# Experts of a mixture in unsplit fp32 on groups of the array's width, with the schedule in two pieces

## The chip, the cores and the metric

The kernel runs on one core of one Trainium2 chip. The time is that of one launch in device microseconds. Before the change it is 1426.45 us, the median of three runs (1423.62 to 1427.33).

## The reference

A transformer step in fp32 for 512 tokens of width 1024, in two blocks. The first is an RWKV-7 mixer beside chunked band attention, with an adaptive norm ahead and an output product behind. The second has a hybrid mixer (state space, forgetting attention, convolution), then a mixture of 32 experts, and a last RMS norm. Only the mixture is changed:

```
p_g = softmax(h @ w_rg + b_rg);  g = argmax(p_g)            # one of 4 groups
top_p, top_i = top_k(softmax(logits of the 8 experts of g), 2)
weights = top_p / sum(top_p) * p_g[g]
for each expert e, on the rows of h that chose it:
    y = (silu(h @ w_gate[e]) * (h @ w_up[e])) @ w_down[e]   # 1024 -> 512 -> 1024
x = x + g_f * sum over a token's two experts of weight * y
out = rms_norm(x) * final_norm_g
```

Each expert has two matrices of 1024 x 512 and one of 512 x 1024 in fp32: 6.29 MB, and 201 MB for all 32. The 512 tokens with two experts each make 1024 rows, which the kernel keeps sorted by expert.

## The kernel before, in words

The kernel is not issued as it is written. A recorder (class `Recorder`, line 209) takes down every instruction with what it reads and writes. A planner (`schedule`, line 613) then simulates the engines with a price for each instruction (`cost`, line 425; 360 GB/s for a transfer) and fixes the order of each engine's queue. `arrange` (line 341) gives every tile a place in one of three areas of the on-chip memory: "f" of 34816 columns in fp32, "r" of 18176 in fp32r, "i" for integers. `build` runs this for the whole kernel as a single piece (line 2611 and following), then emits the instructions. On the chip each engine works through its own queue in that order. Behind it stands a loop for experts with more rows than a window holds; in the profiled execution it has no pass.

**Matmuls in split fp32r.** A factor in fp32 is cut into a high part, rounded to fp32r, and a low part, the difference. A product is then three fp32r matmuls: high by high, low by high, high by low. Each is one instruction on PE.

**Experts.** `expert_code` (line 2397) works on a window of 80 rows of the sorted table `hs`, which holds the 1024 rows transposed, as eight blocks of 128 of the width. It copies the window (ACT, high part; DVE, low part). Then come eight pieces of weights of 128 x 1024 elements (0.5 MB each), gate and up in turn. For each, the high part is copied by ACT or DVE and the low part subtracted by DVE, and PE runs six matmuls with the 80 rows as the stationary operand. After the gate (Tanh on ACT, two fused operations on DVE) the 80 x 512 hidden values are transposed on PE in four parts and split again. Four more pieces hold the down matrix, for another 24 matmuls. The two halves of the result are multiplied by the channel gate `gfb` on DVE, and POOL scatters the rows to the table `Yd` in HBM by row numbers from `sli`; rows past an expert's count have a number out of bounds and are skipped.

```
RAW, HIS, LOS = 14, 6, 6        # line 979
PRE = 14
R.copy(hi, raw)                 # in Rings.split, line 2390
R.tt(lo, raw, hi.bitcast(F32), ALU.subtract)
```

**Weights held.** `Rings` holds 14 pieces in area "f" and 6 high and 6 low parts in area "r". SP loads a piece as soon as the plan has it and the buffer is free, which it is once the two instructions of the split have read it. The first 14 pieces (`PRE`) are loaded ahead of the second mixer's output product.

**Routing.** After the output product the router's logits are transposed (`lg`), and DVE works out group, experts, weights and each row's place in a chain of small instructions. One-hot matrices (`SS`, compared with the row `iota`) and PE give the token numbers in sorted order. POOL gathers eight blocks of 128 rows of the normalized x from HBM (`Xd`), and PE transposes them into `hs`. Expert 0 needs the first block only, expert 1 rows up to 592, the others possibly all.

**The end.** The last two experts are staggered (`AHEAD`, line 981). The result of expert 31 doesn't go through HBM: selection matrices (`selt`, split) times its rows are added to x in PSUM by 24 matmuls. The rows of the others are gathered from `Yd` by POOL, two gathers for each block of 128 tokens. Then come the last norm and the writes of the output.

## Time and profile before

| | us |
|---|---|
| median of 3 runs | 1426.45 |
| lowest, highest | 1423.62, 1427.33 |
| the profiled execution, its own time | 1425.2 |
| its span in the trace | 1423.4 |
| PE busy, PEld busy | 1323.5, 921.0 |
| DVE busy, ACT busy, POOL busy | 1195.8, 834.7, 191.1 |
| weight pieces loaded by SP | 384 of 512 KB |

PE is TensorE's matmuls, PEld its weight loads (they may overlap), DVE VectorE, ACT ScalarE, POOL GpSimd and SP SyncE, which only issues transfers here. The profile is one execution. The span runs from its first to its last instruction, and times in it count from its start. Experts fill the span from about 790 to 1395 us. An fp32 matmul shows as two instructions, an fp32r matmul as one, and both show as "f32" in the shapes; the areas tell them apart ("areaf" is area "f", "arear" area "r"). Nearly all instructions have line 965, where the planned instructions are emitted.

### The profile page before, as it was taken

Reading aid. Unit: us, or ns where it says so; the run is one execution under the profiler, and the core shown is the slowest. Engines: PE = TensorE matmul, PEld = TensorE weight load, DVE = VectorE, ACT = ScalarE, POOL = GpSimd, SP = SyncE. Lnnn points to the kernel's source line nnn. Section 1 sums busy time; section 2 is a strip of 40 time slices with the busy share of each in tenths; the row PEclk is TensorE's granted clock in tenths of the full one; section 3 lists DMA queues with packets and bytes.
Section 4 is the critical chain, followed back from the end, with each engine's and each line's share of the span. In section 5 each row is a group of like instructions: output and inputs, shape, how many; then the busy total and the mean of one; then the engine's idle time right before and its main releaser. Section 6 shows DMA issues by size and latency. Waiting matters only on the chain. (4 is left out here: it accounts for less than half of the span.)

```text
span 1423.4 us, 21185 instructions
## 1 busy us (share of the span) xinstructions
PE 1323.5 (93%) x7400; PEld 921.0 (65%) x7400; DVE 1195.8 (84%) x2183; ACT 834.7 (59%) x1327; POOL 191.1 (13%) x126
## 2 busy tenths in 40 slices
PE   5999999999989989999998899999999999999993
PEld 2766566676757888878886556666556565555552
DVE  5496966679789474999947889999999999999995
ACT  5454634456484254366723578876766677667662
POOL 0000000000001000000101201221523710001123
PEclk8999999999999999999998799999999999999997
DMA  9734766400205511000534689999999999999955
GB/s 334 283 99 147 248 249 222 141 16 17 74 17 164 190 54 55 26 15 2 196 131 148 210 292 364 371 354 364 345 354 357 345 356 359 345 344 339 354 189 182
DMA packets 90739, 307.74 MB, mean 216 GB/s; under 512 B 12034, under 2 KB 15490, under 8 KB 89604
## 3 DMA queue, kind: packets, MB, share of 16 engines
q1 hardware_dynamic: 85252, 293.75, 56.8%
q0 software_dynamic: 5376, 12.59, 2.5%
q8 instruction: 59, 0.97, 0.3%
q14 instruction: 52, 0.43, 0.1%
HBM read 293.72 MB, written 18.87 MB: 220 GB/s over the span
## 5 line engine op out<-in xcount | busy, mean ns | idle before, releaser
L965 PE MATMUL ps<-arear 128*80 128x512 f32 (+3 forms) x4435 | 1063.1, 391 | 44.3 <-DVE areaf L965 17.5
L965 PEld LDWEIGHTS ps<-arear 128*80 128x80 f32 (+1 forms) x4435 | 701.7, 171 | 334.3 <-issue 32.0
L965 ACT ACTIVATE arear<-areaf 128x1024 fp32r<-128x1024 f32 (+7 forms) x542 | 496.8, 944 | 275.2 <-PE ps L965 203.1
L965 DVE TENSOR_TENSOR arear<-areaf,arear 128x1024 fp32r<-128x1024 f32 (+5 forms) x560 | 598.3, 1105 | 50.5 <-PE ps L965 21.5
L965 PE MATMUL ps<-areaf 128*32 128x128 f32 (+18 forms) x2965 | 340.5, 315 | 34.8 <-DVE areaf L965 23.3
L965 PEld LDWEIGHTS ps<-areaf 128*128 128x128 f32 (+7 forms) x2965 | 233.0, 144 | 146.9 <-issue 49.9
L957 POOL DMA_INDIRECT yscr<-areaf,areai x32 | 134.2, 4194 | 434.6 <-DVE areaf L965 404.8
L965 ACT ACTIVATE areaf<-ps 128x512 f32<-128x512 f32 (+7 forms) x294 | 118.6, 421 | 121.1 <-PE ps L965 108.7
L965 ACT ACTIVATE areaf<-areaf 128x512 f32<-128x512 f32 (+9 forms) x246 | 121.4, 512 | 105.9 <-DVE areaf L965 96.2
L965 DVE TENSOR_TENSOR areaf<-ps,areaf 128x512 f32<-128x512 f32 (+6 forms) x245 | 123.4, 513 | 13.4 <-PE ps L965 9.9
L965 DVE SCALAR_TENSOR_TENSOR areaf<-areaf 128x512 f32<-128x512 f32 (+6 forms) x190 | 108.2, 598 | 20.5 <-ACT areaf L965 18.0
L965 DVE TENSOR_TENSOR areaf<-areaf 128x512 f32<-128x512 f32 (+12 forms) x235 | 102.4, 450 | 9.9 <-ACT areaf L965 6.2
L965 DVE SCALAR_TENSOR_TENSOR areaf<-ps,areaf 128x511 f32<-128x511 f32 (+8 forms) x116 | 56.7, 502 | 44.7 <-PE ps L965 39.1
L965 ACT ACTIVATE areaf<-ps,areaf 128x128 f32<-128x128 f32 (+3 forms) x109 | 53.6, 517 | 42.2 <-PE ps L965 24.5
L965 POOL MEMSET areaf<- 128x512 f32 (+10 forms) x53 | 17.2, 331 | 427.8 <-DVE areaf L965 201.4
L965 POOL TENSOR_TENSOR areaf<-areaf 128x4 f32<-128x4 f32 (+2 forms) x21 | 19.9, 971 | 317.4 <-DVE areaf L965 301.7
L965 DVE TENSOR_SCALAR areaf<-areaf 128x256 f32<-128x256 f32 (+12 forms) x192 | 48.1, 280 | 9.8 <-ACT areaf L965 4.3
L965 DVE CAST arear<-areaf 128x1024 fp32r<-128x1024 f32 (+3 forms) x69 | 39.0, 568 | 13.4 <-PE ps L965 12.3
L965 DVE SCALAR_TENSOR_TENSOR areaf<-areaf,ps 80x512 f32<-80x512 f32 (+1 forms) x72 | 48.7, 677 | 0.1
L965 ACT ACT_TABLE_LOAD x35 | 44.9, 1283 | 1.3 <-PEq L2570 0.7
L965 DVE COPY areaf<-ps 32x128 f32<-32x128 f32 (+10 forms) x51 | 19.0, 375 | 23.4 <-ACT areaf L965 12.2
L965 ACT ACTIVATE arear<-ps 128x320 fp32r<-128x320 f32 (+1 forms) x36 | 14.8, 417 | 30.2 <-PE ps L965 30.1
(30 smaller groups left out, 182.1 us busy)
## 6 DMA issues: line engine op xcount, KB each, us to landing
areaf<-in_wx_dram SPq DMA_DIRECT2D x384, 512.0 KB, 5.6
areaf<-in_wada_dram SPq DMA_DIRECT2D x56, 512.0 KB, 4.6
areaf<-in_win_c_dram SPq DMA_DIRECT2D x43, 512.0 KB, 4.5
areaf<-in_wada_dram SPq DMA_DIRECT2D x8, 1024.0 KB, 8.2
areaf<-in_wout_dram SPq DMA_DIRECT2D x16, 512.0 KB, 4.1
areaf<-in_xt_dram SPq DMA_DIRECT2D x16, 256.0 KB, 3.5
yscr<-areaf SPq DMA_DIRECT2D x8, 512.0 KB, 8.2
areaf<-in_win_c_dram SPq DMA_DIRECT2D x24, 128.0 KB, 7.1
```

The lines of the kernel that those rows point to most:

```text
L957: self.emitted[i] = self.nc.gpsimd.indirect_dma_start(un(a[0]), bass.IndirectOffsetOnAxis(ap=un(k["idx"]), axis=0), un(k["in_"]), None, bo ...
L965: self.emitted[i] = getattr(getattr(self.nc, eng), op)(*[un(v) for v in a], **{n: un(v) for n, v in k.items()})
```

## The change

- Experts run in unsplit fp32: no copies, no subtractions, no high and low rings. Each window grows from 80 to 96 rows and is treated as a group of 64 and a group of 32.
- The group of 64 rows is the stationary operand of two matmuls that stand side by side in PE's columns: up in columns 0 to 63 and gate in 64 to 127, each over 512 columns of weights. The down product puts its two halves of 512 side by side likewise.
- The group of 32 rows stands four times side by side, each over 256 columns: both halves of up and of gate, then the four quarters of the down product.
- Results lie on 128 partitions as half and quarter rows. They are scattered by two scatters with their own tables `sl2` and `sl4`, in rows of 512 and 256 elements. The channel gate is spread accordingly (`g2`, `g4`).
- The last expert (31) keeps whole rows for its down product: a 64- and a 32-column matmul into the same bank, and one table `sl1`.
- The router's counting and the one-hot products, and the final selection, are in fp32 instead of fp32r.
- The schedule is cut: `trace` ends once `lg`, the transposed x and the writes to `Xd` are recorded, and `moe` is recorded, planned and emitted as a second piece. For it the columns of area "r" become an fp32 area "g", which holds `hs`, pieces and the last rows.
- The ring of weights is 30 pieces: the 14 loaded in the first piece, 8 in "g", 8 in "f". A piece's buffer is free once PE has read it.
- The planner's rate of transfers becomes 395 GB/s, and its price of a scatter smaller.

```diff
-RAW, HIS, LOS = 14, 6, 6
-PRE = 14
+PRE, MOREW = 14, "g" * 8 + "f" * 8
+RATE = 395.0
-WIN = 80
+WIN = 96
-R_WIDTH = 52992 - F_WIDTH
+R_WIDTH = 52928 - F_WIDTH
...
-    loaded = [rings.load(T["wx"][p]) for p in pieces[:PRE]]
+    loaded = []
+    for p in expert_pieces()[1][:PRE]:
+        loaded.append(R.tile([128, 1024], F32, "xraw"))
+        R.sync.dma_start(loaded[-1], T["wx"][p])
...
+    return dict(C={k: C[k] for k in keep}, loaded=loaded, lg=lg, xs=xs_, Xd=Xd, G3=G3, SH3=SH3, gf=A["gf"][0:64], nhalf=nhalf)
+def moe(R, T, S):
...
-    tid = R.tile([128, NT, 2], F32R, "tid")
+    tid = R.tile([128, NT, 2], F32, "tid")
...
-        gh, gl = R.tile([WIN, 1024], F32R, "ygh"), R.tile([WIN, 1024], F32R, "ygl")
...
-                R.tensor.matmul(p, lhsT=hi, rhs=gh[:, c], start=False, stop=False)
-                R.tensor.matmul(p, lhsT=hi, rhs=gl[:, c], start=False, stop=False)
-                R.tensor.matmul(p, lhsT=lo, rhs=gh[:, c], start=False, stop=(e == NEXP - 1))
+                R.tensor.matmul(p, lhsT=places[e, t], rhs=ys[:, c], start=False, stop=(e == NEXP - 1))
...
-def expert_code(R, C, hs, Yd, rings, gfb):
+def expert_code(R, C, hs, Yd, rings, g2, g4):
+    up, gate = slice(0, 64), slice(64, 128)
+    quarters = [slice(32 * g, 32 * g + 32) for g in range(4)]
...
-        R.scalar.activation(whi, a, AF.Copy)
-        R.vector.tensor_tensor(wlo, b, whi.bitcast(F32), ALU.subtract)
-        p = [bank("pg")[0:WIN], bank("pu")[0:WIN]]
-        for q in range(8):
-            hi, lo = rings.split(piece(q))
...
-                R.tensor.matmul(p[u], lhsT=whi[:, k], rhs=a, start=(k == 0), stop=False)
-                R.tensor.matmul(p[u], lhsT=wlo[:, k], rhs=a, start=False, stop=False)
-                R.tensor.matmul(p[u], lhsT=whi[:, k], rhs=b, start=False, stop=(k == KD - 1))
+        p, p4 = bank("pg"), bank("pg4")[:, 0:256]
+        for q in range(0, 8, 2):
+            g, u = piece(q), piece(q + 1)
             for kk in range(2):
+                k, c = q + kk, 512 * kk
+                with R.together():
+                    for o, w in ((up, u), (gate, g)):
+                        mm(p[o], lhsT=hw[:, k, 0:64], rhs=w[:, c:c + 512], start=(k == 0), stop=(k == KD - 1), tile_position=(0, o.start))
+            for kk in range(2):
+                k = q + kk
+                with R.together():
+                    for n, o in enumerate(quarters):
+                        c = 512 * kk + 256 * (n % 2)
+                        mm(p4[o], lhsT=hw[:, k, 64:96], rhs=(u, g)[n // 2][:, c:c + 256], start=(k == 0), stop=(k == KD - 1), tile_position=(0, o.start))
...
+        if whole:
+            py = [bank("py")[0:WIN], bank("py")[0:WIN]]
+            for k in range(4):
+                w = piece(8 + k)
+                for n in range(2):
+                    with R.together():
+                        for o, l in zip((slice(0, 64), slice(64, WIN)), part(k)):
+                            mm(py[n][o], lhsT=l, rhs=w[:, 512 * n:512 * n + 512], start=(k == 0), stop=(k == 3), tile_position=(0, o.start))
...
+        R.tt(ys, py, g2, ALU.mult)
+        R.tt(ys4, py4, g4, ALU.mult)
+        R.scatter(Yd.rearrange("r (h c) -> (r h) c", h=2), idx[0], ys, 2047)
+        R.scatter(Yd.rearrange("r (h c) -> (r h) c", h=4), idx[1], ys4, 4095)
...
+        areas = {"f": areas["f"], "g": pool.tile([128, R_WIDTH], F32, name="areag", tag="arear"), "i": areas["i"]}
+        R1, S = phase(lambda R, S: moe(R, T, S), S)
```

## Rows read from the trace of the kernel before

**Rows 1.** The page's first part: busy us (share of the span) and count by engine

```profile
PE 1323.5 (93%) x7400; PEld 921.0 (65%) x7400; DVE 1195.8 (84%) x2183; ACT 834.7 (59%) x1327; POOL 191.1 (13%) x126
```

**Rows 2.** Stretches: length, busy of each engine, PE's clock, DMA share, GB/s

```profile
700.00:720.00 20.00, 19.18 (x126) 16.62 (x126) 17.25 (x38) 9.58 (x22) 4.04 (x5) 1.00 0.98 385
780.00:800.00 20.00, 16.80 (x62) 12.80 (x63) 17.16 (x58) 6.05 (x9) 6.33 (x4) 0.57 0.39 130
860.00:920.00 60.00, 59.87 (x266) 37.06 (x266) 59.69 (x62) 48.56 (x52) 13.02 (x3) 1.00 0.98 371
860.00:1380.00 520.00, 501.39 (x2191) 311.29 (x2191) 510.50 (x551) 370.04 (x407) 127.69 (x28) 1.00 0.94 348
```

**Rows 3.** SP's waits (us, times, longest), then the loads of the weights

```profile
SPq L965 <- DVE arear L965: 576.7, 383, 37.7
SPq L965 <- DVE areaf L965: 352.1, 52, 55.1
...
L965 SPq DMA_DIRECT2D areaf<-in_wx_dram x384: 327/328/977, 685.5 to 1364.9; - x192
...
  ACT arear L965: 5.7, 8
...
DMA to landing us min/median/max: 3.1/5.6/10.2
```

**Rows 4.** PE in order of time: start us, us until the last ends, shape, count

```profile
810.82 0.47 PE L965 MATMUL ps<-areaf 80*128 80x80 f32 x4 [0.16 <-DVE areaf L965]
...
860.13 0.44 PE L965 MATMUL ps<-areaf 80*128 80x80 f32 x4
...
1384.70 1.88 PE L965 MATMUL ps<-areaf 128*128 128x512 f32 x4
1388.00 0.50 PE L965 MATMUL ps<-areaf 80*128 80x80 f32 x4 [1.42 <-DVE areaf L965]
1389.02 6.03 PE L965 MATMUL ps<-arear 128*80 128x512 f32 x24 [0.53 <-ACT arear L965]
...
1395.82 1.62 PE L965 MATMUL ps<-arear 80*128 80x512 f32 x5
...
1397.74 4.89 PE L965 MATMUL ps<-arear 80*128 80x512 f32 x19
```

**Rows 5.** Instructions by form: count, busy us, mean ns, idle before

```profile
L965 PE MATMUL ps<-arear 128*80 128x512 f32 x2304 | 556.8, 399 | 17.6 <-ACT arear L965 7.1 <-DVE arear L965 6.3 <-DVE areaf L965 3.2
L965 DVE TENSOR_TENSOR arear<-areaf,arear 128x1024 fp32r<-128x1024 f32 x447 | 526.9, 1215 | 39.4 <-PE ps L965 19.7 <-ACT arear L965 13.7 <-issue 5.0
L965 DVE TENSOR_TENSOR areaf<-ps,areaf 80x512 f32<-80x512 f32 x64 | 43.3, 680 | 2.7 <-PE ps L965 2.7
L965 DVE SCALAR_TENSOR_TENSOR areaf<-areaf,ps 80x512 f32<-80x512 f32 x64 | 43.3, 676 | 0.1
L965 DVE TENSOR_TENSOR arear<-areaf,arear 128x640 fp32r<-128x640 f32 x32 | 26.1, 815 | 0.0
...
L965 PEld LDWEIGHTS ps<-areaf 128*32 128x32 f32 x960 | 23.8, 112 | 36.6 <-issue 21.1 <-DVE areaf L965 7.4 <-ACT areaf L965 3.1
L965 PEld LDWEIGHTS ps<-areaf 128*64 128x64 f32 x416 | 23.5, 137 | 9.4 <-issue 5.5 <-ACT areaf L965 2.4 <-DVE areaf L965 1.1
L965 DVE TENSOR_TENSOR arear<-ps,arear 128x320 fp32r<-128x320 f32 x32 | 15.4, 481 | 1.2 <-ACT arear L965 1.1
```

**Rows 6.** PE in order of time, in earlier stages with column groups

```profile
139.97 0.48 PE L965 MATMUL ps<-arear 128*128 128x512 f32 x1
140.38 4.50 PE L965 MATMUL ps<-areaf 128*32 128x512 f32 x40
144.81 0.97 PE L965 MATMUL ps<-arear 128*128 128x512 f32 x3
...
173.87 1.42 PE L965 MATMUL ps<-areaf 128*64 128x128 f32 x12
...
375.90 0.66 PE L965 MATMUL ps<-areaf 128*64 128x128 f32 x8
```

**Rows 7.** PE's weight loads in the stretch from 140 us, first and last

```profile
140.83 0.13 PEld L965 LDWEIGHTS ps<-areaf 128*32 128x32 f32 x4 [0.30 <-issue]
...
143.83 0.13 PEld L965 LDWEIGHTS ps<-areaf 128*32 128x32 f32 x4 [0.30 <-issue]
```

**Rows 8.** POOL in order of time: gathers of x, last scatter, last gathers

```profile
780.56 3.18 POOL L962 DMA_INDIRECT areaf<-xscr,areai  x1 [9.93 <-DVE arear L965]
...
816.67 0.94 POOL L962 DMA_INDIRECT areaf<-xscr,areai  x1 [0.30 <-issue]
...
1384.18 0.91 POOL L957 DMA_INDIRECT yscr<-areaf,areai  x1 [8.18 <-DVE areaf L965]
1387.71 0.98 POOL L962 DMA_INDIRECT areaf<-yscr,areai  x1 [2.62 <-issue]
...
1398.09 0.94 POOL L962 DMA_INDIRECT areaf<-yscr,areai  x1 [0.30 <-issue]
```

**Rows 9.** DVE and SP at the start of routing, in order of time

```profile
765.99 0.75 DVE L965 TENSOR_SCALAR areaf<-areaf 128x1024 f32<-128x1024 f32 x1
...
776.71 0.47 DVE L965 TENSOR_SCALAR arear<-areaf 128x128 fp32r<-128x128 f32 x2
...
734.31 0.33 SPq L965 DMA_DIRECT2D areaf<-in_iota_dram  x1
...
766.77 3.38 SPq L965 DMA_DIRECT2D xscr<-areaf  x4
```

More of the change, by code (lines that the diff above doesn't have):

```diff
@@ L360, in arrange @@
         where = list(self.where) if self.where else [0] * count
-        for area in areas:
+        for area in areas or self.areas:
             width = self.areas[area].shape[1]
@@ L2069, in trace @@
         return
-    order = sorted([(e, h) for e in range(NEXP) for h in range(2)], key=lambda x: x[0] + (AHEAD if x[1] and x[0] >= AHEAD_FROM else 0.5 * x[1]))
-    pieces = [(e, q) for e, h in order for q in (range(8, 12) if h else range(8))]
-    rings = Rings(R, RAW, HIS, LOS)
-    KR = {}
-    for k in ("ones", "tris"):
-        KR[k] = R.tile([128, 128], F32R, "KR")
-        R.copy(KR[k], C[k])
-    loaded = [rings.load(T["wx"][p]) for p in pieces[:PRE]]
+    loaded = []
+    for p in expert_pieces()[1][:PRE]:
+        loaded.append(R.tile([128, 1024], F32, "xraw"))
+        R.sync.dma_start(loaded[-1], T["wx"][p])
     plg = [mmps("lg")[0:36, 0:256] for _ in HALF]
@@ L2123, in trace, with expert_pieces, mmps, spread @@
         R.sync.dma_start(Xd[128 * t:128 * t + 128], xn)
+    keep = ("ident", "ones", "desc", "iota", "slot", "place2", "part2", "place4", "part4", "tris")
+    return dict(C={k: C[k] for k in keep}, loaded=loaded, lg=lg, xs=xs_, Xd=Xd, G3=G3, SH3=SH3, gf=A["gf"][0:64], nhalf=nhalf)
+def expert_pieces():
+    order = sorted([(e, h) for e in range(NEXP) for h in range(2)], key=lambda x: x[0] + (AHEAD if x[1] and x[0] >= AHEAD_FROM else 0.5 * x[1]))
+    return order, [(e, q) for e, h in order for q in (range(8, 12) if h else range(8))]
+def moe(R, T, S):
+    C, lg, xs_, Xd, G3, SH3, nhalf = (S[k] for k in ("C", "lg", "xs", "Xd", "G3", "SH3", "nhalf"))
+    HS = (slice(0, 64), slice(64, 128))
+    order, pieces = expert_pieces()
+    rings = Rings(R, S["loaded"], MOREW)
+    Yd = R.dram(T["yscr"], "Yd")
+    def mmps(name):
+        return R.tile([128, 512], F32, name, "ps")
+    def spread(r, name):
+        o = R.tile([128, 1024], F32, name)
+        for q in range(2):
+            p = mmps("sp")
+            R.tensor.matmul(p, lhsT=C["ident"][0:64, 32 * q:32 * q + 1].to_broadcast([64, 128]), rhs=r, start=True, stop=True)
+            R.copy(o[:, 512 * q:512 * q + 512], p)
+        return o
     def t_(shape, name, dt=F32):
@@ L2385, in load, with __init__ @@
[L2385 to L2397 removed]
+    def __init__(self, R, loaded, more):
+        self.R, self.ring, self.at = R, list(loaded) + [None] * len(more), len(loaded)
+        self.area = [None] * len(loaded) + list(more)
@@ new lines, in expert @@
+        if start is None:
+            R.scalar.activation(hw, rows, AF.Copy)
+        else:
+            R.scalar.activation(hw, rows.dyn(R.load("scalar", start, top, after=last[0]), window), AF.Copy)
+            last[0] = len(R.ops) - 1
+        p, p4 = bank("pg"), bank("pg4")[:, 0:256]
+        for q in range(0, 8, 2):
+            g, u = piece(q), piece(q + 1)
+            for kk in range(2):
+                k, c = q + kk, 512 * kk
[8 more added lines that the diff above has]
+                        mm(p4[o], lhsT=hw[:, k, 64:96], rhs=(u, g)[n // 2][:, c:c + 256], start=(k == 0), stop=(k == KD - 1), tile_position=(0, o.start))
@@ new lines, in expert @@
+        py, py4 = bank("py"), bank("py4")[:, 0:256]
+        for pair in (0, 2):
+            w = [piece(8 + k) for k in (pair, pair + 1)]
+            for k in (pair, pair + 1):
+                with R.together():
+                    for n, o in enumerate((up, gate)):
+                        mm(py[o], lhsT=part(k)[0], rhs=w[k - pair][:, 512 * n:512 * n + 512], start=(k == 0), stop=(k == 3), tile_position=(0, o.start))
+            for k in (pair, pair + 1):
+                with R.together():
+                    for n, o in enumerate(quarters):
+                        mm(py4[o], lhsT=part(k)[1], rhs=w[k - pair][:, 256 * n:256 * n + 256], start=(k == 0), stop=(k == 3), tile_position=(0, o.start))
@@ L2521, in replace @@
                 order = sorted(R.order, key=lambda i: key[i])
-                for area in areas:
+                for area in list(areas):
                     new = [perm[i] for i in order] if perm else order
```

176 lines of the change are left out of this document (84 added, 92 removed).

## The prediction

> **What bounds the kernel now.** I read the page's busy times first, then the stretches of the expert stage, then the waits of the weight loads, then instructions by form. The page says that PE is busy for 93% of the span and DVE for 84% [rows 1]. Those shares are averages over stages, so the stage decides. From 860 to 920 us PE is busy 59.87 of 60 us, DVE 59.69, and the DMA engines 98% at 371 GB/s [rows 2]: three resources look full at once. Two rows separate them. SP's queue waited 576.7 us for a DVE instruction that writes area "r" (the low-part subtraction, which gives a weight buffer back), while ACT waited for a weight load only 8 times, 5.7 us in all, and a load landed a median 5.6 us after its issue [rows 3]. With about 1.45 us from one load to the next (60 us x 371 GB/s / 0.524 MB = 42 pieces in 60 us), 5.6 us is four pieces in flight; the other ten of the 14 buffers hold data that is waiting to be split. So the transfers wait for the consumers.
>
> The period of one expert is read from the transposes of its hidden rows: the third expert's stand at 860.13 us, the thirty-second's at 1388.00 [rows 4], so 527.9 / 29 = 18.2 us. DVE's own work for an expert is 12 x 526.9/447 + 26.1/32 + 2 x 43.3/64 + 2 x 43.3/64 + 15.4/32 = 14.1 + 0.8 + 1.35 + 1.35 + 0.5 = 18.1 us [rows 5]. PE's: 266 instructions in the 60 us, 76 for an expert, are 3.5 experts, 17.1 us each. DVE sets the period and PE stands one microsecond behind it. That is the heart of the forecast: the change clears DVE, and what it gives PE decides how much of that is seen.
>
> **PE's work for an expert after.** The 72 fp32r matmuls (17.4 us by 72 x 556.8/2304 [rows 5]) go. In their place stand 12 groups of two 64-column matmuls of 512 (8 for gate and up, 4 for down) and 12 groups of four 32-column matmuls of 256. An fp32 matmul is two instructions: 56 pieces of the ada weights give 112 matmuls, and their form has 224. The trace of before has four-way groups of width 512: 40 instructions, ten rounds of four, from 140.38 to the next matmul's start at 144.81, 0.443 us a round [rows 6]. The four run side by side, since alone one such pass costs nearly as much: four 128-column passes took 1.88 us [rows 4]. Two-way groups of 64 columns are there only at width 128: 8 instructions in 0.66 us at 375.90, against 12 mostly one after another in 1.42 us at 173.87 [rows 6]. Without the 0.27 us in which a last one drains, that is 0.39 us for 8 against 1.15 for 12, so pairs do overlap.
> - 24 rounds of 512: 24 x 0.443 = 10.63 us. 24 rounds of 256, at half: 5.32. Together 15.95 us.
> - 6 transposes instead of 4: four take 0.44 us [rows 4], so 0.66.
> - Changes between the two group widths, and to the transposes. Entering the four-way stretch took 0.41 us from one start to the next (139.97 to 140.38) where an fp32r matmul takes 0.24: 0.17 us a change, an upper bound. The ten rounds of 0.443 hold one change themselves. The planner may alternate every two steps (16 changes) or gather them (6). I take 12, of which the rounds' price covers 5, at about 0.12: 0.8 us.
> Sum 17.4 us. Bounds: 24 x 0.43 + 24 x 0.215 + 0.44 + 0.2 = 16.1 from below, and 15.95 + 0.66 + 11 x 0.17 = 18.5 from above. So PE's own work does not fall; the period falls from 18.2 to 17.4 because DVE no longer sets it.
>
> Here the Trainium skill speaks against the change. Its page "TensorE: Matmul & The Clock Gate" (Part 3, The mechanism) says that a weight load overlaps matmuls in flight only when its row group differs, and column groups all share the rows. The trace disagrees for four-way groups of 512: each set of four loads takes 0.13 us and starts within the running round, and the rounds stay at 0.43 to 0.44 [rows 7]. By the rule the sum would be that of the third rival.
>
> **DVE and ACT after.** No splits are left. DVE has per expert two multiplications of 512 and 256 and four fused ones on 64 rows, by 0.68 us for a 512 some 4 us; ACT one window copy, two Tanh, one copy. Both hide behind 17.4 us of PE.
>
> **Transfers.** An expert reads 12 x 0.524 = 6.29 MB and writes 0.13 MB; at the 371 GB/s of the full stretch 17.3 us, at the 385 of 700 to 720 us 16.7 [rows 2]. Nearly PE's period, but 16 more pieces can be loaded before the first expert runs: 16 x 1.4 = 22 us of work done ahead, 0.8 us an expert, so I charge nothing. If the rate stayed at the stage's mean of 348 it would be 18.45, 29 x 18.45 - 22 = 513 us against 505: 8 us. Two scatters an expert instead of one, 0.9 us on POOL when undisturbed [rows 8], lie beside PE.
>
> **The start.** Cutting the schedule puts every phase-two instruction behind all of phase one on its engine. On DVE four scalings of x by 0.74 us stand among the routing steps before [rows 9]; now they stand ahead, but their time is spent either way: +1 us. On SP the load of iota was issued at 734.31, its landing long over; now it follows the four writes of x at 766.77 to 770.2 and lands 3.3 us or more later, while DVE needed it at 776.71 [rows 9]: 0 to 4, taken +2. The first token block's one-hot products become two instructions each: +1. All four us are on the path to the first gather at 780.56. On the other side the low-part subtractions no longer stand between the routing steps, and gathers that came as late as 816.67 [rows 8] can be issued earlier. PE's clock was 0.57 of full from 780 to 800 [rows 2], and I expect the same for the first expert. Before, the third expert's transposes came 49.3 us after the first's at 810.82 [rows 4]; at 17.4 a period it is 34.8, a gain of 14.5. Less the 4: 10 us gained (bounds -4 and +20). Third transposes at 850.
>
> **The end.** From the last expert's transposes to the end of the span 35.4 us. Its 24 down matmuls took 6.03 us; now 8 groups hold a 64- and a 32-column matmul of 512. Side by side 16 rounds, 7.1 us (+1); if the unlike widths take turns 32 rounds of 0.43 and 15 changes of 0.13, 15.7 (+9.7). A change of width cost something wherever it shows, so I take +8. The eight final sums in fp32 take 16 x 0.43 = 6.9 us against 6.8 before (24 from 1395.82 on, the last ending at 1402.63, two identity passes between), and the split of the last rows, about 0.5 us of the path, goes: 0. The gathers of the other rows, 1387.71 to 1398.09 [rows 8], fit beside the longer product. Tail 44 us.
>
> **Sum.** 850 + 29 x 17.4 + 44 = 1398.6 us of span. The profiled execution took 1425.2 for its span of 1423.4, so 1400.4; the median of the runs lies 1.25 above that execution, less than my terms are sure to. Forecast 1400 us, own range 1380 to 1420.
>
> **Rivals.**
> - PE cheaper than that, chance 0.20. The planner gathers equal widths, a period 16.4, and the last product runs side by side (tail 37): 850 + 476 + 37 = 1363, time 1365. For it: rounds of 0.43 inside the stretch. Against: pieces arrive in pairs, which invites alternation.
> - First piece disturbed, chance 0.12. The 14 preloaded pieces have no reader in phase one, so its plan sees no use that would date them and may load them earlier than 685.5 [rows 3], holding 14336 of the 34816 columns while the mixer needs them; loads already waited 352.1 us for areas that DVE had yet to free [rows 3]. Between 10 and 40 us lost: 1410 to 1440, middle 1425. Against: the expert splits and rings leave that piece too.
> - Slower: weight loads show between rounds, chance 0.10. A load of 32 columns is 23.8/960 = 0.025 us of PEld, one of 64 23.5/416 = 0.056 [rows 5]. Two or four exposed in each of 48 rounds: 24 x 0.113 + 24 x 0.10 = 5.1 us, period 22.5, 850 + 652 + 44, time 1548. It decides early: from a period of 18.3, (1423.4 - 44 - 850) / 29, on, which is 0.9 us an expert or 18 ns a round more than I sum, the kernel is slower than before. For it: pairs of 64 at width 512 and fours at 256 at full clock have no row of their own here. Against: rows 7.
> - The change doesn't do what it says, chance 0.03: pairs take turns, 24 x 0.443 = 10.6 us more, period 28, time 1708. Against: the pairs of rows 6.
>
> **Chances and range.** Forecast 0.55. A difference under about 0.3% (4 us) is what a measurement of this kernel can't tell from none. Faster: 0.53 of the forecast, all 0.20 of the first rival, 0.06 of the second: 0.79. Same: 0.02 and 0.04: 0.06. Slower: 0.02 of the second, 0.10 and 0.03: 0.15. The range 1357 to 1434 holds the forecast, most of the first two rivals and the near edge of the third.
>
> **What would show it.** Transposes of neighbouring experts 17.4 us apart with PE near full and DVE under a third; SP waiting for PE and no longer for DVE; third transposes near 850; rounds of 0.43 to 0.45 and 0.21 to 0.23. Wrong if PE waits for weights (transfers bind), if PEld shows before each round, if the first gather comes after 790, or if the router's logits are late: then the cut cost phase one.

## The result, and the profile after

The changed kernel takes 1448.23 us (median of 4 runs, 1441.82 to 1450.44) against 1426.89 for the one before, measured beside it: slower by a ratio of 1.0141, 95% interval 1.0098 to 1.0183. The forecast was 1400, so it missed by 48 us and had the sign wrong. The profiled execution took 1450.44, its span 1448.6.

The experts do what was forecast. The page's busy times, SP's waits, and the stretches (length, then busy time of PE, PEld, DVE, ACT, POOL, PE's clock, DMA share, GB/s) beside [rows 1 to 3]:

```profile
PE 1344.5 (93%) x9815; PEld 801.3 (55%) x9815; DVE 740.2 (51%) x1801; ACT 492.5 (34%) x982; POOL 113.2 (8%) x157
```

```profile
SPq L971 <- PE ps L971: 556.5, 210, 12.2
```

```profile
780.00:800.00 20.00, 9.39 (x34) 7.34 (x34) 18.20 (x100) 1.72 (x5) 0.00 (x0) 0.56 0.62 236
800.00:820.00 20.00, 19.21 (x89) 18.39 (x90) 7.88 (x36) 2.15 (x6) 4.91 (x5) 0.50 0.43 132
820.00:840.00 20.00, 18.44 (x101) 10.10 (x104) 3.69 (x9) 5.52 (x11) 1.87 (x2) 0.74 0.34 105
860.00:920.00 60.00, 56.87 (x488) 21.99 (x488) 11.44 (x22) 10.33 (x19) 5.44 (x6) 0.97 0.96 373
920.00:1060.00 140.00, 136.85 (x1236) 53.92 (x1232) 26.79 (x50) 18.46 (x32) 14.73 (x15) 1.00 1.00 372
...
1200.00:1340.00 140.00, 132.42 (x1125) 51.46 (x1123) 24.20 (x47) 16.82 (x30) 17.68 (x18) 0.99 0.92 346
```

DVE is out of the way (a fifth of the stretch from 920 us, where it was full), and SP's queue waits for PE to give buffers back, no longer for a subtraction. But in the three stretches from 780 to 840 us PE's granted clock is 0.56, 0.50 and 0.74 of full, with PE busy for 9.4, 19.2 and 18.4 of 20 us, and the DMA engines are half idle. The clock is at the lower of its two levels for 48 us on end, twice as long as before the change (first the kernel before, then the one after):

```profile
773.40:797.30 23.90, 18.07 (x65) 14.83 (x66) 20.89 (x87) 5.17 (x9) 6.33 (x4) 0.50 0.27 89
```

```profile
782.60:830.40 47.80, 36.34 (x154) 31.51 (x156) 24.94 (x122) 6.27 (x14) 4.91 (x5) 0.50 0.46 162
```

What happened there is read from PE, DVE, POOL and ACT in order of time (start us, us until the last ends, shapes, count). Again the kernel before comes first, then the one after:

```profile
715.24 32.27 PE L965 MATMUL ps<-arear 128*128 128x512 f32 x177 [0.82 <-DVE areaf L965]
747.85 7.68 PE L965 MATMUL ps<-arear 128*128 128x256 f32 x61 [0.34 <-DVE areaf L965]
755.47 14.34 PE L965 MATMUL ps<-areaf 128*36 128x256 f32 x80
...
777.04 8.10 PE L965 MATMUL ps<-arear 128*128 128x2 f32 x34 [2.33 <-DVE arear L965]
...
765.34 0.31 DVE L965 TENSOR_TENSOR areaf<-ps,areaf 128x144 f32<-128x144 f32 x1 [1.14 <-POOL areaf L965]
```

```profile
726.64 32.91 PE L971 MATMUL ps<-arear 128*128 128x512 f32 x180
759.90 7.69 PE L971 MATMUL ps<-arear 128*128 128x256 f32 x61 [0.34 <-DVE areaf L971]
767.42 11.89 PE L971 MATMUL ps<-areaf 128*128 128x1 f32 x74
...
796.11 20.97 PE L971 MATMUL ps<-areaf 128*128 128x2 f32 x96 [0.22 <-DVE areaf L971]
...
779.89 0.31 DVE L971 TENSOR_TENSOR areaf<-ps,areaf 128x144 f32<-128x144 f32 x1 [5.57 <-PE ps L971]
...
805.67 1.16 POOL L968 DMA_INDIRECT areaf<-xscr,areai  x1 [33.89 <-DVE areai L971]
...
846.03 0.94 POOL L968 DMA_INDIRECT areaf<-xscr,areai  x1 [9.77 <-PE ps L971]
...
846.38 0.49 ACT L971 ACTIVATE areaf<-ps 128x384 f32<-128x384 f32 x1
...
869.60 0.49 ACT L971 ACTIVATE areaf<-ps 128x384 f32<-128x384 f32 x1 [1.33 <-PE ps L971]
...
892.39 0.49 ACT L971 ACTIVATE areaf<-ps 128x384 f32<-128x384 f32 x1 [1.95 <-PE ps L971]
...
1401.28 3.69 PE L971 MATMUL ps<-areaf 64*128 64x64 f32 x12
1404.90 7.99 PE L971 MATMUL ps<-areag,areaf 128*64 128x512 f32 x16
...
1420.73 8.92 PE L971 MATMUL ps<-areaf 96*128 96x512 f32 x20
```

The second output product's 512-column run ends 12 us later. A row bears the shape of its first instruction: the one that opens with 128x1 sums holds x's transposes, which stand in front of the logits' own. DVE's first step on the logits (128x144) comes at 779.9 for 765.3. The fp32 token products (128x2, two instructions each) run in a block of some 96 instructions, and the first and last gather come at 805.7 and 846.0 for 780.6 and 816.7 [rows 8]. ACT's copies of the first three experts' transposes stand 23.2 and 22.8 us apart, not 17.4. The transposes themselves begin at 842.1, 867.7 and 891.8; the last at 1401.3, so the period is (1401.3 - 891.8) / 29 = 17.57 us, and the tail 47.3.

So the span is 891.8 + 29 x 17.57 + 47.3, against a forecast of 850 + 29 x 17.4 + 44. Of the 50 us by which the span misses the forecast, 41.8 are the start.

### The profile page after: what moved, and what is told of

It is laid out like the page before. It is cut to its first block, busy times and chain, and to the rows that moved or that the text cites. A ratio compares the mean times of both kernels' runs of the same rounds, so it can differ in the third digit from the quotient of the medians.

```text
span 1448.6 us, 24736 instructions
## 1 busy us (share of the span) xinstructions
PE 1344.5 (93%) x9815; PEld 801.3 (55%) x9815; DVE 740.2 (51%) x1801; ACT 492.5 (34%) x982; POOL 113.2 (8%) x157
## 5 line engine op out<-in xcount | busy, mean ns | idle before, releaser
L971 PE MATMUL ps<-areaf 128*32 128x256 f32 (+13 forms) x6535 | 780.4, 389 | 67.1 <-DVE areaf L971 47.9
L971 PEld LDWEIGHTS ps<-areaf 128*32 128x32 f32 (+4 forms) x6535 | 410.9, 136 | 442.9 <-issue 234.1
L971 PE MATMUL ps<-arear 128*128 128x512 f32 (+4 forms) x2040 | 485.1, 384 | 16.2 <-DVE areaf L971 10.4
L971 PEld LDWEIGHTS ps<-arear 128*128 128x128 f32 x2040 | 348.0, 193 | 97.6 <-issue 16.5
L971 ACT ACTIVATE areaf<-ps 128x384 f32<-128x384 f32 (+7 forms) x352 | 146.0, 429 | 481.9 <-PE ps L971 468.3
L971 DVE TENSOR_TENSOR areaf<-ps,areaf 128x256 f32<-128x256 f32 (+5 forms) x245 | 115.4, 480 | 138.4 <-PE ps L971 126.5
L971 ACT ACTIVATE arear<-areaf 128x1024 fp32r<-128x1024 f32 (+3 forms) x163 | 117.7, 740 | 138.2 <-PE ps L971 104.0
L971 ACT ACTIVATE areaf<-areaf 128x512 f32<-128x512 f32 (+8 forms) x240 | 113.5, 490 | 141.8 <-DVE areaf L971 134.0
L971 PE MATMUL ps<-areag,areaf 128*32 128x256 f32 (+1 forms) x1240 | 151.9, 457 | 1.9 <-ACT areaf L971 1.9
L971 DVE TENSOR_TENSOR arear<-areaf,arear 128x1024 fp32r<-128x1024 f32 (+4 forms) x142 | 123.7, 881 | 39.4 <-PE ps L971 20.0
L971 POOL MEMSET areaf<- 128x512 f32 (+9 forms) x52 | 15.8, 308 | 376.5 <-PE ps L971 178.0
```

Of the source, the lines that this page charges most:

```text
L971: self.emitted[i] = getattr(getattr(self.nc, eng), op)(*[un(v) for v in a], **{n: un(v) for n, v in k.items()})
```

## The experiments

All are edits of the changed kernel unless they say otherwise. The table has what each profiled execution showed: start of the last 512-column matmul of the second output product (P), DVE's first step on the logits (L), first, third and last transposes of experts (T1, T3, T32), span; then the median of the runs and the ratio to the kernel before with its interval.

| run | P | L | T1 | T3 | T32 | span | median | ratio |
|---|---|---|---|---|---|---|---|---|
| before | 748.1 | 765.3 | 810.8 | 860.1 | 1388.0 | 1423.4 | 1426.9 | |
| after | 760.1 | 779.9 | 842.1 | 891.8 | 1401.3 | 1448.6 | 1448.2 | 1.0141 (1.0098-1.0183) |
| e2 | 754.3 | 774.1 | 830.0 | 886.7 | 1446.5 | 1493.4 | 1491.5 | 1.0432 (1.0382-1.0482) |
| e3 | 758.7 | 778.4 | 837.3 | 885.2 | 1395.2 | 1443.8 | 1443.7 | 1.0117 (1.0089-1.0146) |
| e4 | 755.5 | 775.3 | 837.7 | 887.3 | 1396.9 | 1435.3 | 1437.7 | 1.0089 (1.0059-1.0119) |
| e5 | 762.5 | 782.3 | 832.1 | 893.3 | 1420.3 | 1473.1 | 1468.1 | 1.0272 (1.0243-1.0300) |
| e6 | 755.6 | 775.3 | 839.8 | 890.9 | 1419.0 | 1467.6 | 1463.8 | 1.0250 (1.0232-1.0269) |
| e7 | 754.9 | 774.7 | 860.4 | 906.6 | 1419.0 | 1465.4 | 1468.5 | 1.0304 (1.0275-1.0333) |
| e8 | 757.8 | 777.5 | 850.3 | 902.1 | 1364.0 | 1417.0 | 1419.3 | 0.9944 (0.9924-0.9964) |
| e9 | 770.9 | 790.7 | 842.3 | 892.1 | 1443.6 | 1483.8 | 1485.2 | 1.0402 (1.0378-1.0425) |
| e10 | 756.6 | 776.3 | 836.8 | 884.6 | 1391.7 | 1438.7 | 1440.9 | 1.0094 (1.0070-1.0118) |
| e11 | 769.0 | 784.5 | 849.9 | 904.7 | 1414.2 | 1460.8 | 1463.4 | 1.0249 (1.0231-1.0268) |
| e12 | 760.0 | 773.9 | 846.9 | 891.0 | 1401.0 | 1449.7 | 1452.4 | 1.0174 (1.0153-1.0194) |
| e13 | 767.6 | 779.7 | 853.4 | 897.5 | 1410.2 | 1450.7 | 1452.8 | 1.0184 (1.0157-1.0210) |
| e14 | 750.3 | 768.4 | 814.5 | 864.0 | 1396.9 | 1432.8 | 1432.5 | 1.0031 (1.0011-1.0052) |
| e15 | 757.4 | 774.5 | 817.0 | 865.5 | 1392.8 | 1427.9 | 1432.2 | 1.0042 (1.0023-1.0062) |
| e16 | 744.9 | 762.1 | 829.1 | 872.9 | 1377.9 | 1426.4 | 1429.7 | 1.0018 (1.0004-1.0032) |
| e17 | 744.9 | 762.1 | 819.3 | 873.8 | 1362.9 | 1404.2 | 1406.0 | 0.9874 (0.9824-0.9923) |
| e18 | 749.1 | 766.4 | 821.3 | 865.2 | 1372.8 | 1421.2 | 1423.5 | 0.9963 (0.9945-0.9980) |
| e19 | 746.1 | 763.3 | 814.5 | 861.4 | 1350.0 | 1391.0 | 1394.6 | 0.9780 (0.9757-0.9803) |

After, e4, e6, e7, e8 and e10 share one first piece, and their P is 754.9 to 760.1, mean 756.7. Before, e16, e17, e18 and e19 share another: 744.9 to 749.1, mean 746.6. That is how far executions of one order differ. The loss of phase one (all that stands ahead of the cut) is 10 us in the mean, 12 between the two executions shown above. Where the plan of the experts came out unlike the changed kernel's, times don't compare and the stages are read.

The changed kernel as one piece (e1) was to be the first experiment and has no result. So the new experts in an uncut schedule are untested; e9 and e14 to e16 stand in for it.

**e2, the planner's rate.**

```diff
-RATE = 395.0
+RATE = 360.0
```

> The changed kernel with the planner's rate of transfers back at 360 GB/s from 395. Theory (the cut): the second output product still ends late, its first run of matmuls at 726 or later where before the change it was at 715, and the time is 1448 within 6. Rival (the planner's rate: at 395 GB/s it orders work ahead of loads that come later than it thinks, and phase one waits): that run starts near 715, the logits come 11 us earlier, 1437 us.

P is 754.3: the rival's 12 us didn't come. The experts' own plan got far worse (T3 to T32 559.8 us for 509.5), so the time says nothing of the cut.

**e3, fewer preloads.**

```diff
-PRE, MOREW = 14, "g" * 8 + "f" * 8
+PRE, MOREW = 4, "g" * 8 + "f" * 18
```

> The changed kernel with 4 pieces of weights loaded in the first piece of the schedule instead of 14, the ring of 30 kept. Theory (the preloads have no reader in the first piece, so they are not dated by a use and take columns and transfer time from the mixer): the logits come 8 to 11 us earlier, the rest follows, 1437 to 1440 us unless the experts then miss the ten pieces (10 x 1.4 = 14 us more, 1451). Rival (the preloads are innocent): logits at 779 within 3, and 1448 to 1462 us.

The logits came at 778.4: the preloads are innocent of phase one, and the ten pieces were not missed either (T3 to T32 is 510.0). The time, 1443.7, is 4 us below the rival's range, since the third transposes came 106.8 us behind the logits and not 111.9.

**e4, the last product in pairs.**

```diff
...
-                        for o, l in zip((slice(0, 64), slice(64, WIN)), part(k)):
+                        q = 256 + 64 * (k % 2) + 32 * (k // 2)
+                        for o, l in zip((up, gate), (part(k)[0], d[:, q:q + 64])):
```

> The changed kernel, but the last expert's down product uses two 64-column matmuls side by side (the group of 32 rows widened to 64 columns, the added columns belonging to rows whose result isn't read) in place of a 64- and a 32-column one. Theory (unlike widths take turns): the product from 1404.9 to 1420.7, 15.8 us, falls to 16 rounds x 0.44 = 7.1 us, and the time by 8.5 us to 1440. Rival (transfers or the gathers set the end, so the turns were hidden): the product falls and the time stays at 1448 within 3.

The product fell to 7.1 us, two rows of 3.6, where it took from 1404.90 to 1420.73 before, 15.8. PE's weight loads (the last two rows) start within the running rounds, 0.43 us apart:

```profile
1400.55 3.65 PE L971 MATMUL ps<-areag,areaf 128*64 128x512 f32 x16
1404.03 3.60 PE L971 MATMUL ps<-areaf 128*64 128x512 f32 x16
...
1401.03 0.14 PEld L971 LDWEIGHTS ps<-areag,areaf 128*64 128x64 f32 x2 [0.29 <-issue]
1401.46 0.14 PEld L971 LDWEIGHTS ps<-areag,areaf 128*64 128x64 f32 x2 [0.29 <-issue]
```

The tail is 38.4 us for 47.3. Here unlike widths take turns, and like ones stand side by side. That agrees with the Trainium skill, "TensorEngine Tiling (Array Packing)" (Tiling Modes, Key Properties): a change of the tiling mode drains the engine, a change of the tile within a mode does not.

**e5, another order of the first piece** (the second keeps 40 us).

```diff
-ROUNDS = ((40000, 25000),)
+ROUNDS1, ROUNDS2 = ((30000, 25000),), ((40000, 25000),)
...
```

> The changed kernel, cut as it is, but the first piece planned with another lead for the dates at which the planner places loaded tiles (30 us in place of 40); the second piece's own lead is as before. It gives a first piece with another order of the same work. Theory (the cut as such costs nothing in phase one; the first piece just got a worse order than the single piece of before had): the second output product's matmuls begin their last long run near 715 and the router's logits are copied near 766, 10 to 12 us earlier than in the changed kernel, and third transposes come as much earlier: 1436 us within 5. Rival (any cut plan is late, because what stood behind the cut no longer fills its gaps): logits at 775 or later, 1443 to 1452 us.

P is 762.5, later than in the changed kernel, and the experts came out slower too (18.2 us each), which puts the time above both ranges. The theory that the planner just had bad luck with one parameter got no support here.

**e6, one-hots in bf16.** The token number is 128 t + slot in two columns, added after the product.

```diff
-    tid = R.tile([128, NT, 2], F32, "tid")
+    tid = R.tile([128, NT, 2], BF16, "tid")
...
-                a = R.tile([128, hi - lo], F32, "SS")
+                a = R.tile([128, hi - lo], BF16, "SS")
```

> The changed kernel with the one-hot matrices and token numbers in bf16 (both exact; a number is the sum of two columns), so a token product is one matmul instruction and not two. Theory (the fp32 products at half clock make the gathers late): from the first DVE step on the logits (779.9 in the changed kernel) to the first gather 18 us and not 25.8, and the last gather, 66.1 behind it, at 56; third transposes 8 to 10 us earlier, 1439 us. Rival (DVE's chain with the tables for the overflow in between sets the gathers): 24 to 26 and 62 to 66 us, time 1444 to 1450.

The first and last gather came 21.5 and 56.9 us behind the logits, but the third transposes 115.6. This plan put the second block's gather 13 us behind the first, and PE was busy for 3.36 and 8.26 us of the two stretches from 780 to 820. Inconclusive; e18 repeats it in another order.

**e7, blocks in turn.** Around the one-hots, products, cast and gathers of each block:

```diff
...
+        with R.in_turn():
...
```

> The changed kernel with the token blocks written in turn: all of the first block's one-hots, products, cast and gather keep their order ahead of the wider blocks'. Theory (the second block's 256-wide one-hots and their 64 product instructions came first): logits to first gather 15 to 18 us and not 25.8, to the last gather 50 to 56 and not 66; third transposes 8 to 12 us earlier, 1436 to 1440 us. Rival (what is late is the work of all blocks together at half clock): the first gather comes early, the last as before, third transposes within 3 of 891.8 less what phase one gives, 1444 to 1450 us.

The first gather came early (19.2 us behind the logits), the last as late as before (69.6), and the third transposes 20 us later behind the logits (131.9 for 111.9): the products and most transposes of all blocks now went ahead of the first expert's. An early first gather alone gives nothing back.

**e8, PE's share and the transfers'.** The bank of the 32-row products is set to zero, and their matmuls for gate and up are left out.

```diff
+        R.vector.memset(p4, 0.0)
...
-                    for n, o in enumerate(quarters):
-                        c = 512 * kk + 256 * (n % 2)
-                        mm(p4[o], lhsT=hw[:, k, 64:96], ...
...
```

> The changed kernel without the gate and up products of the group of 32 rows (their bank is set to zero, so rows 65 to 96 of a window get none of the experts' work). It takes 16 of 24 rounds of 256 columns from PE. Theory (PE sets the period of 17.3 us in the first half of the stage, and transfers stand just behind it): PE's own work falls by 16 x 0.22 = 3.5 us to 13.8, but the transfers hold the period at 6.29 MB / 372 GB/s = 16.9 us, so a gain of 0.4 an expert there; time 1430 to 1440. Rival (transfers are far from binding): period 13.8 to 14.5, time 1350 to 1365.

The period is 15.9 us from the third to the last transposes, 16.8 to the thirtieth (the last two experts come together): the rival falls. Transfers run faster than in [rows 2] (e8's stage to the thirtieth expert, then its fastest stretch):

```profile
902.00:1357.00 455.00, 405.29 (x2397) 136.85 (x2398) 100.95 (x201) 62.67 (x110) 53.20 (x54) 0.92 0.99 387
1200.00:1340.00 140.00, 129.31 (x793) 44.95 (x797) 29.63 (x57) 21.58 (x37) 16.75 (x17) 0.96 1.03 408
```

At 408 GB/s an expert's 6.29 MB take 15.4 us. But over the whole stage the DMA engines are busy for 0.99 of the time at 387 GB/s, and PE, with a third less to do for gate and up, gets no further than 16.8 us an expert. It waits 41.5 us there for DVE and 6.5 for loads, so transfers aren't shown to be the one bound. What e8 shows is that they can keep up with 16.8 us; how far below that they could go is open. The time is 11 us below the theory's range, which had 16.9 us an expert to the end.

**e9, the cut alone, on the kernel before.** The function ends at the same place and the rest is planned as a second piece.

```diff
-PRE = 14
+PRE = 6
...
+    return dict(C={k: C[k] for k in keep}, loaded=loaded, lg=lg, xs=xs_, Xd=Xd, ...
...
+def moe(R, T, S):
...
+    rings.rings["raw"], rings.at["raw"] = list(loaded), len(loaded)
```

> The kernel before with the cut alone: the old split fp32r experts on rows of 80, recorded, planned and emitted in two pieces at the same place as in the changed kernel; 6 of the 14 pieces of weights are loaded in the first piece, the other 8 in the second. Theory (the cut costs the start, whatever the experts are): the second output product ends 7 us or more later than before the change, the step from its end to the first DVE step on the logits grows from 17 to 20 us, the gathers follow later, and the time is 15 to 45 us above before: 1440 to 1470 us. Rival (the new experts and their fp32 products cost the start, the cut does not): 1426 within 6.

The third transposes come at 892.1, as in the changed kernel, without a single new expert instruction. P is 23 us late, and the step to the logits is 19.8 us for 17.2, as in the changed kernel. The stage is slower too (19.0 us an expert): the ring became the list of the 6 loaded pieces, where the expectation has 14. So the time, 1485, 15 us above the theory's range, tells nothing of the cut; P and the step to the logits do.

**e10, matmuls that were to keep the clock up.**

```diff
+    pw = mmps("warm")
+    for q in range(20):
+        R.tensor.matmul(pw[:, 0:256], lhsT=xs_[q % 4][:, 0:128], rhs=xs_[q % 4][:, 256:512], start=True, stop=True)
```

> The changed kernel with 20 fp32 matmuls of 128 x 256 added whose result nobody reads, 19 of them planned in PE's idle time between the logits and the first token products. In the changed kernel PE's granted clock was 0.56 from 780 to 800 us, 0.50 from 800 to 820 and 0.74 from 820 to 840. Theory (PE at half clock on the token products and on the transposes of the gathered rows sets the start): the clock stays at 0.9 or more from 780 on, the 98 token product instructions take 11 to 13 us and not 21, and from the first DVE step on the logits to the third expert's transposes it is 97 to 102 us and not 112; time 1434 to 1440. Rival (routing steps, gathers and copies set it): the clock rises and the stretch stays at 108 to 114 us, or the added matmuls delay the routing; time 1445 to 1452.

```profile
778.40:788.70 10.30, 9.02 (x23) 6.55 (x23) 8.74 (x53) 1.06 (x4) 0.00 (x0) 0.50 0.99 384
788.70:798.90 10.20, 10.20 (x73) 9.61 (x71) 10.10 (x51) 0.00 (x0) 0.00 (x0) 1.00 0.17 70
798.90:826.20 27.30, 25.83 (x105) 20.10 (x106) 6.54 (x24) 5.25 (x11) 4.91 (x5) 0.50 0.36 116
...
800.00:820.00 20.00, 18.53 (x85) 16.93 (x84) 5.54 (x15) 5.25 (x11) 4.91 (x5) 0.50 0.50 159
```

The added matmuls run from 778.7 to 794.6. The clock was at half (0.50) up to 788.7 in spite of them, full for 10.2 us, and fell again at 798.9, after 10.2 us in which PE had no gap and the last 4 of which were products of two columns. From 800 to 820 it stood at 0.50 with PE busy for 18.53 of 20 us. So the clock was not kept. Logits to third transposes: 108.3 us for 111.9, in the rival's range, with a time of 1440.9 between the two. What a full clock through all the products would be worth is not shown.

**e11, logits first.**

```diff
+                with R.in_turn():
+                    R.tensor.matmul(plg[h], lhsT=wr[:, m], rhs=x1[m][:, part], start=(m == 0), stop=(m == KD - 1))
...
+    with R.in_turn():
+        prs = mmps("rs")
...
```

> The changed kernel with the router's logits, their transposes and sums written in turn, so that they no longer stand behind the transposes of x on PE. Theory (the cut made the logits nothing special: whatever ends the first piece is as urgent): from the start of the last 512-column matmul of the second output product to the first DVE step on the logits 17 us as before the change and not 19.8; time 2 to 4 us less, 1445. Rival (x and its writes are needed as early as the logits, for the first gather): the 3 us come back as a wait of the first gather for the writes of x, time 1448 within 3.

P to L is 15.5 us for 19.8, so the 3 us are real. The first gather kept 1.9 of these 4.3 us (43.6 us behind P for 45.6), and it waited for DVE, not for the writes of x. The new order of the first piece ended the product at 769.0, and its plan of the experts differs, so the time tells nothing.

**e12, first piece cut out of a plan of the whole**, and **e13, three edits together** (e12, e10, e4).

```diff
-        R1, S = phase(lambda R, _: trace(R, T, off, ...
+        R1, S = phase(both, first=first)
```

`both` records `trace` and `moe` as one for the planner, and the instructions of `trace` are then emitted in that order.

> The changed kernel, emitted in the same two pieces, but the first piece's order and places come from a plan of the whole kernel, cut afterwards (the preloaded pieces, the logits and the writes of x are then ranked and dated by what the experts need). The second piece is planned as in the changed kernel. Theory (phase one got late because it was planned without what follows): the last 512-column matmul of the second output product starts at 745 to 750 us, as before the change (748), and not at 755 to 771 as in every cut kernel so far; time 8 to 14 us below the changed kernel, 1437. Rival (what is emitted behind the cut is what phase one misses, or the longer area left to it): 755 or later, time 1446 to 1455.

> Three of the edits together on the changed kernel: the first piece ordered by a plan of the whole, 20 matmuls that keep PE's clock up while the routing runs, and the last product in two 64-column matmuls. If each removes its own stretch of the path and they add up: 10 + 4 + 9 us, 1425 us, level with the kernel before (1427). If the first piece's order gives nothing: 1435. If all three were one and the same slack: 1438 or more.

Both theories miss, and e12 is in its rival's range. P is 760.0 and 767.6. In e12 the first gather comes 35.7 us behind the logits: the load of iota was issued at 786.2, behind the writes of x, and DVE waited for it.

```profile
795.75 0.35 DVE L971 TENSOR_SCALAR areaf<-areaf 128x256 f32<-128x256 f32 x1 [5.89 <-DMA areaf<-in_iota_dram]
```

What followed behind the cut was known to this plan, and it was as late as the others. In e13 the tail is 40.5 us, so that remedy holds; the rest is lost to the order.

**e14 and e15, the kernel before in another order** (e15 with 30000).

```diff
-ROUNDS = ((40000, 25000),)
+ROUNDS = ((60000, 25000),)
```

> The kernel before, in one piece and with its old experts, planned anew with 60 us for 40 as the lead for dates of loaded tiles. Theory (a new order of phase one is what the change paid for, cut or not): its second output product's last 512-column matmul starts at 754 to 771 us as in the eight cut kernels, not at 748, and the time is 6 to 20 us above before, 1433 to 1446. Rival (the cut is what costs): 748 within 4, and 1427 within 5.

> The same with a lead of 30 us. Theory (a new order): 754 to 771 us and a time of 1433 or more. Rival (the cut): 748 within 4, 1427 within 5.

P is 750.3, in the rival's range, and 757.4, in the theory's; T3 is 864.0 and 865.5, the times 0.3% and 0.4% longer, between the two forecasts. A new order can cost phase one something without any cut: e14's hardly more than the spread of one order, e15's as much as the earlier cut orders.

**e16, the cut in the order of before.** The places and the order of the first piece's instructions are those of the kernel before, written out as lists. **e18** is the same with e6's edit.

```diff
-        R1, S = phase(lambda R, _: trace(R, T, off, ...))
+        R1, S = phase(lambda R, _: trace(R, T, off, ...), given=PLAN1)
```

> The changed kernel, cut as it is, but the first piece runs in exactly the order of the kernel before, in the same places (one preloaded piece lies elsewhere). The second piece is planned anew as ever. Theory (the new order of phase one costs 8 us, the cut itself only what stands behind it): last 512-column matmul of the second output product at 748 within 3, logits near 766, third transposes near 878, time 1437 within 4. Rival (what the cut takes out of phase one or puts into it in emission): 754 or later, 1446 or more.

> The run in the order of before with the one-hot matrices and token numbers in bf16, so half the token product instructions; nothing else. There the first DVE step on the logits came at 762.1 us and the third transposes at 872.9, 110.8 us later; before the change it was 94.8. Theory (the doubled token products at half clock are the rest of the start's loss; they took about 21 us in one block in front of the gathered rows' transposes): 97 to 101 us, third transposes 860 to 863, time 1418 within 5. Rival (PE then idles where the products stood, since gathers and copies come one behind the other, as in the bf16 run with the first piece's new order, 115.6): 108 to 116 us, time 1428 or more.

PE and DVE of e16, then stretches of e18:

```profile
744.63 7.68 PE L976 MATMUL ps<-arear 128*128 128x256 f32 x61 [0.34 <-DVE areaf L976]
752.25 14.34 PE L976 MATMUL ps<-areaf 128*36 128x256 f32 x80
...
780.99 19.16 PE L976 MATMUL ps<-areaf 128*128 128x2 f32 x88 [2.18 <-DVE areaf L976]
...
762.12 0.31 DVE L976 TENSOR_TENSOR areaf<-ps,areaf 128x144 f32<-128x144 f32 x1 [1.14 <-POOL areaf L976]
```

```profile
780.00:800.00 20.00, 4.33 (x46) 2.96 (x46) 16.73 (x83) 0.71 (x2) 4.64 (x5) 0.50 0.75 281
800.00:820.00 20.00, 17.07 (x118) 7.04 (x120) 6.54 (x16) 6.27 (x13) 2.50 (x3) 0.73 0.48 154
820.00:840.00 20.00, 18.35 (x146) 8.96 (x140) 8.62 (x24) 7.25 (x17) 2.97 (x3) 1.00 1.00 399
```

With the old order the cut costs phase one nothing: the product's end and the step to the logits are those of before, and the time falls by 18.6 us, to within 0.2% of before and 3 us below the theory's range. The block of products remains: 88 instructions in 19.16 us, and 110.8 us from the logits to the third transposes. Halving those instructions (e18) takes 12 us off that stretch (98.8, against 94.8 before the change), in the middle of the theory. DVE's widest one-hots take 0.42 us in both, so it isn't bf16 on DVE that gained. e19 against e17, below, gives 13.5 (98.1 for 111.6); e6, in the changed kernel's order, had given nothing. The time, 1423.5, is half a microsecond above its range; this execution's phase one ended 4.2 us later than e16's.

**e17 and e19, remedies together.** e17 is e16 with the edits of e4 and e10 and the lines below for the second piece; e19 has e6's edit too, with 500.0 and 60000.

```diff
-RATE = 395.0
+RATE = 420.0
-ROUNDS = ((40000, 25000),)
+ROUNDS = ((30000, 25000),)
...
```

> The kernel of the run before this one with the last product in two 64-column matmuls, 20 matmuls that keep PE's clock up while the routing runs, and the second piece planned at 420 GB/s with a lead of 30 us, so that the plan of the experts is set by PE. If the order of before gives 8 us, the pairs 9, the kept clock 4, and the period stays at 17.0 us throughout in place of a mean of 17.57: 1448 - 8 - 9 - 4 - 16 = 1411 us, below before (1427). If the transfers hold the late experts at 18 us and more whatever the order: 1425 to 1432.

> The candidate (order of before, two 64-column matmuls in the last product, 20 matmuls that keep the clock up, experts planned with fast transfers, here 500 GB/s and a lead of 60 us) with bf16 one-hots as well. If the halved products shorten the start by 10 to 14 us and period and tail stay at 16.9 and 41: third transposes 860 to 864, time 1392 to 1396. If the start stays at 110 us behind the logits: 1404 to 1408, as without them.

```profile
920.00:1060.00 140.00, 140.00 (x1276) 55.41 (x1274) 28.86 (x52) 19.84 (x34) 16.72 (x17) 1.00 1.00 382
1200.00:1340.00 140.00, 140.00 (x1250) 54.78 (x1248) 27.78 (x51) 18.51 (x32) 16.72 (x17) 1.00 0.99 376
```

These are e17's stretches. PE has no gap left, and the period is (1362.9 - 873.8) / 29 = 16.87 us throughout. The changed kernel's late experts, with PE at 132.42 of 140, were slow by their order and not by transfers: in that stretch PE waited for the gate of an expert on DVE and ACT (the row below and 1.4 us), and for no load.

```profile
PE ps L971 <- DVE areaf L971: 6.2, 6, 2.0
```

e17 takes 1406.0 us, 5 below its forecast. e19 takes 1394.6, in its range and 2.2% less than the kernel before: T3 861.4, period 16.85, tail 41.0. It beats both kernels. The added matmuls gave nothing in e17, whose first three experts stand as late behind the logits as e16's: over half of them ran only from 828.8 us on, among the first experts.

## Why the prediction was wrong

**"The start" is the step that failed**, with +41.8 us against 850. It had three errors.
- "Cutting the schedule puts every phase-two instruction behind all of phase one ... All four us": phase one itself was charged nothing. Its new order ended the output product 12 us later here, 10 in the mean, and put the x transposes ahead of the logits, 2.6 us (19.8 for 17.2). This was the rival "first piece disturbed", for another reason than the one given: not the preloads (e3). e16 shows that the order, with the places that go with it, is the whole of it. Against the mean of 746.6, a new order costs 4 and 11 us even uncut (e14, e15); the eight cut orders cost 8 to 24. Why all eight are later than the order of before is open, since e12's, made with what follows in view, was late as well. The +1 for the scalings and +2 for the load of iota were not needed: the first one-hot came 11.6 us behind the logits (791.5), and 11.4 before (776.7 [rows 9]).
- "+1" for the token products as "two instructions each". They are 64 more instructions, most of them at half clock, in front of the gathered rows: from the logits to the first transposes 62.2 us for 45.5. Halving them gives back 12 of these 16.7 in the order of before (e18). In the changed kernel's own order it gave nothing (e6), so there the share of the products is argued, and the other 5 us are open.
- "At 17.4 a period it is 34.8, a gain of 14.5": the 49.3 us between first and third transposes before the change were taken for two periods, though two of 18.2 are 36.4. PE spent 8.8 us of them on other work (transposes of gathered rows, token products) and was idle for 3.6; I dropped that from the sum. It is still there: of 49.7 us after, 6.6 are such transposes and 4.1 idle. The rows are the kernel before's, then the changed one's:

```profile
L965 PE MATMUL ps<-areaf 128*128 128x128 f32 x37 | 7.1, 298 | 2.0 <-ACT areaf L965 2.0
L965 PE MATMUL ps<-arear 128*128 128x2 f32 x14 | 1.7, 250 | 0.0
...
L971 PE MATMUL ps<-areaf 128*128 128x128 f32 x42 | 6.6, 284 | 2.2 <-ACT areag L971 1.7 <-DVE areag L971 0.4 <-DVE areaf L971 0.2
```

12 + 2.6 + 16.7 (first transposes) and 0.4 + 14.5 (the gain that didn't come), less the 4 that was forecast for the cut, are the 41.8 within half a microsecond.

**PE's work and the period: right, by two errors that cancel.** 17.57 measured, 17.4 forecast. PE's own work is 16.87 (e17). I took 12 changes of width an expert; in e17's trace there are about 7 (173 runs of like matmuls in 24.9 experts, 920 to 1340 us). The order of the experts gives 0.7 back. That the forecast met the period is luck.

**Weight loads** did not show between rounds: a pair's 16 rounds took 7.1 us, 0.44 each (e4). Here the trace goes against the rule of the Trainium skill that the prediction weighed ("TensorE: Matmul & The Clock Gate", Part 3, The mechanism).

**Transfers** were charged nothing, rightly: SP waits for PE, and e17's PE has no gap at 16.87. How far below that their own bound lies is open (e8 ran at 16.8).

**The end: right mechanism.** 47.3 for 44. The last product took 15.8 us, the bound named for turns (15.7); I took 8 of its 9.7. The step from the last transposes to that product added 2.6 [rows 4], which I had at nothing.

The prediction's own warning held: "if the first gather comes after 790, or if the router's logits are late".

## What to carry to other kernels

Where a planner orders the work, an edit to one stage re-rolls the order of all the others: compare the untouched stages first, and keep their order fixed (e16) before the edit is judged. When a start is scaled from one kernel to the next, subtract the work that the edit does not touch before dividing by the period. Two matmuls of unlike width (64 and 32 columns here) cost like two in a row where they were meant to stand side by side; padding the narrow one took 8.7 us off 15.8 (e4).

## What the runs showed of the hardware

- PE's granted clock stood at 0.50 while PE was busy for 18.5 to 19.2 of 20 us, with products of two columns (after, e10), and in e10 it fell from full to half behind 10.2 us without a gap. A busy PE was no sign of the full clock here.
- Two column groups of 64 ran a round of 512 columns in 0.43 to 0.44 us with their weight loads inside (e4). A group of 64 and one of 32 took turns: 15.8 us (after) where two of 64 took 7.1 (e4).
- One core's transfers ran at 408 GB/s over 140 us and at 387 over 455 us (e8); the most in [rows 2] was 385.
- Kernels with one and the same order of phase one ended it up to 5 us apart (754.9 to 760.1).
